# Sum of reciprocals: the input's rows laid out over the partitions in another way

## The chip, the cores and the metric

The kernel runs on one core of a Trainium2 chip. The metric is the device time of one execution in microseconds (us). Engines are named as in the profile: PE (TensorE), DVE (VectorE), ACT (ScalarE), POOL (GpSimd) and SP (SyncE), which here only issues DMAs. Sixteen DMA engines move data between the memory of the chip (DRAM) and the 128 partitions of the core's SBUF.

## The reference

```python
def setup_inputs():
    batch, seq, dim = 32, 512, 1024
    return {"x": np.abs(np.random.randn(batch, seq, dim)).astype(np.float32) + 1e-6}

def reference(x):
    return np.sum(1.0 / x, axis=-1).astype(np.float32)
```

There are 32 x 512 = 16,384 rows of 1,024 numbers, 4 KB each, 67.1 MB in all. The result is one number a row, 64 KB.

## The kernel before

Each partition handles 128 of the 16,384 rows. "Row r" below, from 0 to 127, means the r-th row of every partition, that is 128 rows of the input and 0.524 MB. The view `x_v` says which they are: partition p holds the 64 input rows from 64p on as its rows 0 to 63 (a = 0), and the 64 from 8192 + 64p on as its rows 64 to 127 (a = 1). So neighbouring partitions read addresses 256 KB apart, and `HALF` = 64 is a border that no transfer crosses.

SBUF has a ring of R = 46 slots of one row (`ring`). A load of rows goes into their slots as soon as the work on the rows that were there is done. The result of row r is column r of `sums`.

A reciprocal is the square of a reciprocal square root, and the work is spread over the engines in several ways. All that is done, and in which order on each engine, is written out by hand in `PLAN`, a list of tokens of a letter, a row, and a number of rows:

- `D10` loads the next 10 rows (line 169, SP). The tokens give 2, 10, 12, 12, 10 rows to fill the ring, then 10, 10, 10, 8, 8, 4, 5, 5, 4, 4, 3, 2, 2, 2, 1, 1, 1, 1 rows, and at last row 127 in two pieces of half a row.
- `A` is the reciprocal square root of whole rows, in place (line 177, ACT). `C` squares them on ACT, `Z` squares and sums on ACT (line 187), `G` squares on POOL (line 280), `Q` squares and sums on DVE (line 240), `T` sums on DVE (line 283), and `B`, `K`, `M` get the sum of squares from statistics on DVE (lines 255, 265, 270).
- `P`, `U`, `L`, `E`, `R` are a second way for some rows: POOL multiplies the two halves of a row (line 194), PE adds them (line 201), ACT takes the reciprocal square root of the products and squares it (line 211), and DVE multiplies and sums (line 220), since 1/a + 1/b = (a + b)/(ab).
- `O` issues the early stores of result columns (line 157, SP): columns 0 to 31, 32 to 63, 64 to 81, 82 to 98 and 99 to 115. The last store, columns 116 to 127, comes after the whole plan.

The D token that begins at row 56 asks for 10 rows; the loop over `m` cuts it at HALF into 8 and 2. So there are 26 load transfers and 6 stores, all on SP's queue, 32 in all. They take eight completion semaphores in turn, and a transfer waits on SP until the one that had its semaphore before has landed.

Of the kernel before, what the change touches and what calls it, by code (L numbers as in the profile page):

```python
# [11 lines left out]
def kernel(  # L12
# [5 lines left out]
    nc = tc.nc  # L18
    f32 = mybir.dt.float32
    P = 128  # L20
# [1 line left out]
    D = 1024  # L22
    H = D // 2
    F = 128
    HALF = F // 2
    R = 46
    NP = 5
    PIECES = ((127, 0, 512), (127, 512, 512))
    NR = 127
    STATS = ((55, 4, 16), (78, 4, 9),)  # L30
    STORES = (0, 32, 64, 82, 99, 116)
    LATE = ("A", 127)
    S = float(2**17)
    FIT = 1.0 - 2.0**-17
# [28 lines left out]
    mult = mybir.AluOpType.mult  # L63
    add = mybir.AluOpType.add

    x_v = x.flatten_outer_dims().rearrange("(a p f) d -> a p f d", a=2, p=P)
    out_v = out.flatten().rearrange("(a p f) -> a p f", a=2, p=P)

    act_sets = list(get_activation_tables(nc.m.arch).keys())
    nc.scalar.add_instruction(  # L70
# [13 lines left out]
    sums = pool.tile([P, F], f32)  # L84
# [12 lines left out]
    def place(u):  # L97
        return (u, 0, D) if u < NR else PIECES[u - NR]

    def area(u, n=1):  # L100
        r, at, w = place(u)
        if u >= NR:
            w, n = sum(place(i)[2] for i in range(u, u + n)), 1
        return ring[:, r % R : r % R + n, at : at + w]
# [48 lines left out]
    slot, bank = {}, {}  # L153

    def store(lo, hi):
        a, at = divmod(lo, HALF)
        nc.sync.dma_start(out=out_v[a, :, at : at + hi - lo], in_=sums[:, lo:hi])

    with tc.manual_schedule():
        for op, u, n, b in (parse(tok) for tok in PLAN):  # L160
            if op == "D":
                n, u = u, loaded
                while n:
                    r, at, w = place(u)
                    m = min(n, R - r % R, NR - u, HALF - r % HALF) if u < NR else n
                    k = m
                    if u >= NR:
                        w, k = sum(place(i)[2] for i in range(u, u + m)), 1
                    inst = nc.sync.dma_start(  # L169
                        out=area(u, m),  # L170
                        in_=x_v[r // HALF, :, r % HALF : r % HALF + k, at : at + w],
                    )
                    note("SP", inst, writes=rows(u, m))
                    u, n = u + m, n - m
                loaded = u
            elif op in "AC":
                inst = nc.scalar.activation(  # L177
                    out=area(u, n),
                    in_=area(u, n),
                    func=Arsqrt if op == "A" else Square,  # L180
                    scale=FIT if op == "A" else 1.0,
                )
                note("ACT", inst, writes=rows(u, n))
                work[op, u] = inst.ins
            elif op == "Z":
                r = place(u)[0]
                inst = nc.scalar.activation(  # L187
                    out=area(u), in_=area(u), func=Square, accum_out=sums[:, r : r + 1]
                )
                summed.add(r)  # L190
                note("ACT", inst, writes=rows(u))
            elif op == "P":
                slot[u], r = b, u % R
                inst = nc.gpsimd.tensor_tensor(  # L194
                    out=prod[:, b], in0=ring[:, r, :H], in1=ring[:, r, H:], op=mult
                )
                note("POOL", inst, rows(u), [("slot", b)])
            elif op == "U":
                bank[u], r = b, u % R
                for h in range(2):  # L200
                    inst = nc.tensor.matmul(  # L201
                        ps[:, b],
                        lhsT=ident,
                        rhs=ring[:, r, h * H : (h + 1) * H],
                        start=h == 0,
                        stop=h == 1,
                    )
                    note("PE", inst, half(u, h * H), [("bank", b)])
            elif op in "LE":
                pair = prod[:, slot[u]]  # L210
                inst = nc.scalar.activation(  # L211
                    out=pair,
                    in_=pair,
                    func=Arsqrt if op == "L" else Square,
                    scale=S * FIT if op == "L" else 1.0,
                )
                note("ACT", inst, writes=[("slot", slot[u])])
            elif op == "R":
                pair = prod[:, slot[u]]
                inst = nc.vector.tensor_tensor_reduce(  # L220
                    out=pair,
                    in0=pair,
                    in1=ps[:, bank[u]],
                    scale=S,
                    scalar=0.0,
                    op0=mult,
                    op1=add,
                    accum_out=sums[:, u : u + 1],
                )
                note("DVE", inst, [("bank", bank[u])], [("slot", slot[u])])  # L230
            elif op == "Q":
                r, at, w = place(u)
                joined = [u]
                while len(joined) < n:
                    joined += [i for i in range(NR, u) if place(i)[0] == r][-len(joined) :][:1]
                at -= sum(place(i)[2] for i in joined[1:])
                w += sum(place(i)[2] for i in joined[1:])
                row = ring[:, r % R, at : at + w]
                total = sums[:, r : r + 1]
                inst = nc.vector.tensor_tensor_reduce(  # L240
                    out=row,
                    in0=row,
                    in1=row,
                    scale=1.0,
                    scalar=total if r in summed else 0.0,
                    op0=mult,
                    op1=add,
                    accum_out=total,
                )
                summed.add(r)  # L250
                note("DVE", inst, writes=[s for i in joined for s in rows(i)])
            elif op == "B":
                i = stat_rows.index(u)
                for h in range(2):
                    inst = nc.vector.bn_stats(  # L255
                        out=stats[:, i, h], in_=ring[:, u % R, h * H : (h + 1) * H]
                    )
                    note("DVE", inst, reads=half(u, h * H), writes=[("stat", i)])
            elif op in "KM":
                lo, step, n = STATS[u]  # L260
                i = stat_rows.index(lo)
                part = stats[:, i : i + n]
                if op == "K":
                    mean = part[:, :, :, :, 1].rearrange("p f h e -> p (f h e)")
                    inst = nc.scalar.activation(  # L265
                        out=mean, in_=mean, func=Square, scale=float(H // 2) ** 0.5
                    )
                    engine = "ACT"
                else:
                    inst = nc.vector.tensor_reduce(  # L270
                        out=sums[:, lo : lo + step * (n - 1) + 1 : step],
                        in_=part[:, :, :, :, 1:].rearrange("p f h e k -> p f (h e) k"),
                        axis=mybir.AxisListType.XY,
                        op=add,
                    )
                    engine = "DVE"
                note(engine, inst, writes=[("stat", j) for j in range(i, i + n)])
            elif op == "G":
                row = area(u, n)
                inst = nc.gpsimd.tensor_tensor(out=row, in0=row, in1=row, op=mult)  # L280
                note("POOL", inst, writes=rows(u, n))
            elif op == "T":
                inst = nc.vector.tensor_reduce(  # L283
                    out=sums[:, u : u + n],
                    in_=area(u, n),
                    axis=mybir.AxisListType.X,
                    op=add,
                )
                note("DVE", inst, reads=rows(u, n))
            elif op == "O":  # L290
                for lo, hi in zip(STORES, STORES[1:]):
                    store(lo, hi)
        store(STORES[-1], F)
        for i in range(NOPS):
            inst = nc.gpsimd.nop(hint="idle", nofuse=True)
            if i == 0:
                tc.add_manual_dep(
                    inst.ins,
                    work[LATE].name,
                    mybir.DependencyInfo(  # L300
                        mybir.DependencyClass.Sync, mybir.DependencyReason.DATA
                    ),
                    reason="GpSimd idles behind the loads",
                )
# [30 lines left out]
```

## Time and profile before

| | |
|---|---|
| Time, median of 3 runs | 165.95 us (165.87 to 166.01) |
| Time of the profiled execution | 165.94 us |
| Span in its profile, first to last instruction | 164.2 us |
| Outside of the span | 1.74 us |
| Busy: ACT, DVE, POOL, PE | 148.9, 122.1, 97.2, 28.8 us |
| DMA queue of the loads and stores | 4,608 packets, 67.18 MB, 96.3% of 16 engines' span |
| Mean rate over the span | 409 GB/s |

The busy rows count an engine's own instructions; issuing a DMA counts as busy on no engine, and shows in the rows of SP's queue (SPq). A row of a source line gives an operation's shortest, median and longest duration in ns, and when the first and the last of them started. "DMA to landing" is the time from issue to the last byte. A row of the timeline gives start, duration, engine, line, operation and, in brackets, how long the engine was idle before it and what ended that.

### The profile page before, as it was taken

How to read it: one execution, taken by the hardware profiler on the slowest of the kernel's cores; microseconds unless marked ns; L12 is line 12 of the kernel's file. 1: busy time of each engine (PE TensorE's matmuls, PEld its weight loads, DVE VectorE, ACT ScalarE, POOL GpSimd, SP SyncE). 2: the span in 40 equal slices, each digit the busy share in tenths (PEclk: the TensorE clock that was granted, in tenths of full speed). 3: DMA queues.
4: the chain of work that ended last, by engine and by line, in shares of the span. 5: the costliest groups of instructions: out<-in, count | busy, mean ns of one | idle time of the engine just before them, and what ended most of it. 6: DMA issues, size and time to landing. Idle time of an engine off the chain costs nothing.

```text
span 164.2 us, 575 instructions
## 1 busy us (share of the span) xinstructions
PE 28.8 (18%) x48; PEld 10.3 (6%) x48; DVE 122.1 (74%) x148; ACT 148.9 (91%) x138; POOL 97.2 (59%) x47
## 2 busy tenths in 40 slices
PE   0000000000058000000000062000000077797700
PEld 0000000000022000000000020000000022232200
DVE  0000002599389996499999889979999999999994
ACT  3630799899999999999999999999999999999994
POOL 1000224924799399999999999674072695465400
PEclk9999999999999655555555559555555558999995
DMA  5979998899897999999899799999999999999970
GB/s 188 547 319 479 395 563 383 383 515 443 383 469 329 479 479 401 399 471 415 375 495 469 337 495 393 471 407 391 447 413 449 415 435 411 434 408 414 409 257 4
DMA packets 4611, 67.20 MB, mean 409 GB/s; under 512 B 1280, under 2 KB 1280, under 8 KB 2048
## 3 DMA queue, kind: packets, MB, share of 16 engines
q1 hardware_dynamic: 4608, 67.18, 96.3%
q14 instruction: 3, 0.02, 0.0%
HBM read 67.11 MB, written 0.07 MB: 409 GB/s over the span
## 4 chain that ended last, share of the span: by engine, by line
ACT 48%; DMA 42%; DVE 5%; POOL 2%; issue 1%; SPq 0%; DVEq 0%; POOLq 0%
DMA ring<-in_x_dram 42%; ACT ring L177 37%; ACT ring L187 6%; ACT prod L211 5%; DVE sums L283 3%; DVE ring L240 2%; POOL prod L194 2%; SPq L169 0%; DVE stats L255 0%; DVE prod L220 0%; ACT stats L265 0%; DVE sums L240 0%; DVEq L240 0%; POOLq L194 0%; DVEq L330 0%
## 5 line engine op out<-in xcount | busy, mean ns | idle before, releaser
L177 ACT ACTIVATE ring<-ring 128x1024 f32<-128x1024 f32 (+5 forms) x69 | 114.6, 1722 | 12.0 <-DMA ring<-in_x_dram 12.0
L280 POOL TENSOR_TENSOR ring<-ring 128x1024 f32<-128x1024 f32 (+3 forms) x29 | 81.1, 2820 | 48.1 <-ACT ring L177 48.1
L283 DVE TENSOR_REDUCE sums<-ring 128x1 f32<-128x1024 f32 (+3 forms) x30 | 56.8, 1920 | 31.2 <-ACT ring L177 30.9
L201 PE MATMUL ps<-ring,ident 128*128 128x512 f32 x48 | 28.8, 742 | 126.7 <-DMA ring<-in_x_dram 126.7
L240 DVE CUSTOM_DVE_ANT_0 ring<-ring 128x1024 f32<-128x1024 f32 (+1 forms) x20 | 28.8, 1450 | 5.9 <-ACT ring L177 5.8
L255 DVE BATCH_NORM_STATS2 stats<-ring 128x6 f32<-128x512 f32 x50 | 31.2, 680 | 2.6 <-ACT ring L177 2.5
L187 ACT ACTIVATE ring<-ring 128x1024 f32<-128x1024 f32 x21 | 21.9, 1041 | 0.0
L194 POOL TENSOR_TENSOR prod<-ring 128x512 f32<-128x512 f32 x12 | 15.6, 1308 | 9.0 <-DMA ring<-in_x_dram 9.0
L201 PEld LDWEIGHTS ps<-ring,ident 128*128 128x128 f32 x48 | 10.3, 231 | 144.3 <-DMA ring<-in_x_dram 86.5
L211 ACT ACTIVATE prod<-prod 128x512 f32<-128x512 f32 x24 | 14.2, 618 | 0.1
L220 DVE CUSTOM_DVE_ANT_0 prod<-prod,ps 128x512 f32<-128x512 f32 x12 | 7.9, 678 | 0.0
L187 ACT ACTIVATION_READ_ACCUMULATOR ring<-ring 128x1 f32 x21 | 3.9, 187 | 0.0
L70 ACT ACT_TABLE_LOAD x1 | 1.3, 1283 | 0.7 <-PEq L319 0.7
L240 DVE DVE_READ_ACCUMULATOR2_ANT sums<- 128x1 f32 x21 | 1.7, 81 | 0.0
L220 DVE DVE_READ_ACCUMULATOR2_ANT sums<- 128x1 f32 x12 | 1.0, 82 | 0.0
L240 DVE CUSTOM_DVE_ANT_0 ring<-ring,sums 128x512 f32<-128x512 f32 x1 | 0.8, 752 | 0.1
L265 ACT ACTIVATE stats<-stats 128x36 f32<-128x36 f32 (+1 forms) x2 | 0.5, 258 | 0.0
L270 DVE TENSOR_REDUCE sums<-stats 128x9 f32<-128x72 f32 (+1 forms) x2 | 0.5, 248 | 0.0
masks.py:197 POOL MEMSET ident<- 128x128 f32 x1 | 0.2, 205 | 0.3 <-POOLq L319 0.3
masks.py:199 POOL TENSOR_SCALAR_AFFINE_SELECT ident<-ident 128x128 f32<-128x128 f32 x1 | 0.3, 295 | 0.1
L319 POOL MEMSET const-float32-0.0<- 128x1 f32 x1 | 0.1, 99 | 0.2 <-issue 0.2
L319 POOL MEMSET const-bfloat16-1.0<- 128x1 bf16 x1 | 0.1, 102 | 0.0
(2 smaller groups left out, 0.2 us busy)
## 6 DMA issues: line engine op xcount, KB each, us to landing
ring<-in_x_dram SPq DMA_DIRECT2D x4, 5120.0 KB, 34.4
ring<-in_x_dram SPq DMA_DIRECT2D x2, 6144.0 KB, 37.5
ring<-in_x_dram SPq DMA_DIRECT2D x3, 4096.0 KB, 31.1
ring<-in_x_dram SPq DMA_DIRECT2D x3, 2048.0 KB, 35.9
ring<-in_x_dram SPq DMA_DIRECT2D x5, 1024.0 KB, 33.1
ring<-in_x_dram SPq DMA_DIRECT2D x2, 2560.0 KB, 35.2
ring<-in_x_dram SPq DMA_DIRECT2D x4, 512.0 KB, 21.7
ring<-in_x_dram SPq DMA_DIRECT2D x1, 1536.0 KB, 40.3
```

What stands on the lines that cost most here:

```text
L70: nc.scalar.add_instruction(mybir.InstLoadActFuncSet(name=nc.get_next_instruction_name(), act_func_set_id=act_sets.index("abs_reciprocal_s ...
L177: inst = nc.scalar.activation(out=area(u, n), in_=area(u, n), func=Arsqrt if op == "A" else Square, scale=FIT if op == "A" else 1.0,)
L187: inst = nc.scalar.activation(out=area(u), in_=area(u), func=Square, accum_out=sums[:, r : r + 1])
L194: inst = nc.gpsimd.tensor_tensor(out=prod[:, b], in0=ring[:, r, :H], in1=ring[:, r, H:], op=mult)
L201: inst = nc.tensor.matmul(ps[:, b], lhsT=ident, rhs=ring[:, r, h * H : (h + 1) * H], start=h == 0, stop=h == 1,)
L211: inst = nc.scalar.activation(out=pair, in_=pair, func=Arsqrt if op == "L" else Square, scale=S * FIT if op == "L" else 1.0,)
L220: inst = nc.vector.tensor_tensor_reduce(out=pair, in0=pair, in1=ps[:, bank[u]], scale=S, scalar=0.0, op0=mult, op1=add, accum_out=sums[:, ...
L240: inst = nc.vector.tensor_tensor_reduce(out=row, in0=row, in1=row, scale=1.0, scalar=total if r in summed else 0.0, op0=mult, op1=add, acc ...
L255: inst = nc.vector.bn_stats(out=stats[:, i, h], in_=ring[:, u % R, h * H : (h + 1) * H])
L265: inst = nc.scalar.activation(out=mean, in_=mean, func=Square, scale=float(H // 2) ** 0.5)
L280: inst = nc.gpsimd.tensor_tensor(out=row, in0=row, in1=row, op=mult)
L283: inst = nc.vector.tensor_reduce(out=sums[:, u : u + n], in_=area(u, n), axis=mybir.AxisListType.X, op=add,)
```

## The change

The view of the input becomes `(l e f) d -> e l f d` with l = 8, e = 16 and f = 128. The input is seen as 128 pieces of 128 sequent rows (512 KB); partition 8e + l holds piece 16l + e. So the eight partitions 8e to 8e + 7 read pieces that lie 16 pieces (8 MB) apart, and partitions that differ by 8 read pieces next to each other. The output's view is changed alike. The source of a load has now two counted dimensions (16 and 8) ahead of the contiguous run, where it had one (128); the destination is as before.

With the border at row 64 gone, the D token at row 56 is one transfer of 10 rows, which leaves 25 load transfers. The early stores are cut in steps of `PART` = 20 columns up to `DONE` = 116, six in place of five. Loads and stores together stay 32. `PLAN` is the same.

```diff
-    HALF = F // 2
...
-    STORES = (0, 32, 64, 82, 99, 116)
+    DONE = 116
+    PART = 20
...
-    x_v = x.flatten_outer_dims().rearrange("(a p f) d -> a p f d", a=2, p=P)
-    out_v = out.flatten().rearrange("(a p f) -> a p f", a=2, p=P)
+    x_v = x.flatten_outer_dims().rearrange("(l e f) d -> e l f d", l=8, e=P // 8)
+    out_v = out.flatten().rearrange("(l e f) -> e l f", l=8, e=P // 8)
...
     def store(lo, hi):
-        a, at = divmod(lo, HALF)
-        nc.sync.dma_start(out=out_v[a, :, at : at + hi - lo], in_=sums[:, lo:hi])
+        nc.sync.dma_start(out=out_v[:, :, lo:hi], in_=sums[:, lo:hi])
...
-                    m = min(n, R - r % R, NR - u, HALF - r % HALF) if u < NR else n
+                    m = min(n, R - r % R, NR - u) if u < NR else n
...
                     inst = nc.sync.dma_start(
-                        out=area(u, m),
-                        in_=x_v[r // HALF, :, r % HALF : r % HALF + k, at : at + w],
+                        out=area(u, m), in_=x_v[:, :, r : r + k, at : at + w]
                     )
...
             elif op == "O":
-                for lo, hi in zip(STORES, STORES[1:]):
-                    store(lo, hi)
-        store(STORES[-1], F)
+                for c in range(0, DONE, PART):
+                    store(c, min(c + PART, DONE))
+        store(DONE, F)
```

## Prediction

> **What bounds the kernel now.** I read the busy line and the DMA rows of the page first, then the waits of ScalarE (ACT), then the table of stages, then the issue rows of SyncE (SP). The page says that two things are nearly full: the DMA queue and ACT.
>
> ```profile
> PE 28.8 (18%) x48; PEld 10.3 (6%) x48; DVE 122.1 (74%) x148; ACT 148.9 (91%) x138; POOL 97.2 (59%) x47
> ...
> q1 hardware_dynamic: 4608, 67.18, 96.3%
> ```
>
> The reader sees ACT busy for 148.9 of 164.2 us and the 16 DMA engines for 96.3% of the span. Which of them sets the end is told by ACT's first 33 us and its list of waits:
>
> ```profile
> 5.51 1.91 ACT L177 ACTIVATE ring<-ring 128x2048 f32<-128x2048 f32 x1 [3.50 <-DMA ring<-in_x_dram]
> ...
> 17.61 10.91 ACT L177 ACTIVATE ring<-ring 128x2048 f32<-128x2048 f32 x6 [7.96 <-DMA ring<-in_x_dram]
> ...
> 32.15 1.06 ACT L177 ACTIVATE ring<-ring 128x1024 f32<-128x1024 f32 x1 [0.52 <-DMA ring<-in_x_dram]
> ```
> ```profile
> ACT ring L177 <- DMA ring<-in_x_dram: 12.0, 3, 8.0
> ACT L70 <- PEq L319: 0.7, 1, 0.7
> ```
>
> ACT waits for a load three times, for transfers 1 (2 rows), 2 (10 rows) and 3 (12 rows), and never after 32.15. From there it works without a gap to the end: 161.78 - 32.15 = 129.6 us. So a thing that moves the first three landings moves the end by the same amount, and a thing that happens to the loads later costs nothing until they fall behind ACT. They are not far ahead. Here is the table of stages:
>
> ```profile
> 17.60:32.10 14.50, 0.00 (x0) 0.00 (x0) 3.41 (x2) 14.03 (x12) 7.30 (x2) 1.00 1.00 434
> 32.10:60.00 27.90, 5.96 (x8) 2.34 (x8) 23.43 (x20) 27.85 (x21) 18.74 (x9) 0.91 1.00 432
> 60.00:100.00 40.00, 3.73 (x4) 1.18 (x4) 34.93 (x29) 39.97 (x34) 39.66 (x14) 0.51 0.99 425
> 100.00:145.00 45.00, 10.24 (x19) 3.93 (x20) 43.76 (x63) 44.96 (x42) 25.59 (x15) 0.62 1.00 425
> ```
>
> The columns are the stretch, its length, then busy time of PE, PEld, DVE, ACT and POOL, the granted clock, the DMA share and GB/s. The DMA share is 0.99 to 1.00 at 425 to 434 GB/s all the way: ten rows of 0.524 MB land in 17.61 - 5.51 = 12.10 us, 1.21 us a row, or 433 GB/s. The last two pieces, issued at 146.0 and 148.4, need 13.2 and 11.5 us to land, so the last one is there at 159.9, and ACT's last four ARSQRTs (A125 to A128) run back to back:
>
> ```profile
> 157.71 3.03 ACT L177 ACTIVATE ring<-ring 128x1024 f32<-128x1024 f32 x4
> ```
>
> They end at 160.74, and A128, a half row of about 0.6 us, starts at 160.1. So the stream leaves ACT some 0.2 us there. Both are at their limit together.
>
> The third limit is what lies outside both, at the start and at the end: SP's issue.
>
> ```profile
> L169 SPq DMA_DIRECT2D ring<-in_x_dram x26: 327/328/652, 0.7 to 148.4; - x26
> ...
> DMA to landing us min/median/max: 4.8/33.3/56.0
> ```
> ```profile
> L169 SPq DMA_DIRECT2D ring<-in_x_dram x5: 383/427/652, 0.7 to 2.8; - x5
> ```
> ```profile
> L157 SPq DMA_DIRECT2D out_dram<-sums x6: 332/332/348, 150.9 to 161.9; - x6
> L157 SPq EVENT_SEMAPHORE  x4: 17/17/3392, 153.4 to 158.5; - x4
> ...
> DMA to landing us min/median/max: 1.4/5.2/9.1
> ```
>
> The durations are minimum, median and maximum in ns; the middle row is the first five loads alone. The first load goes out at 0.74 and lands 4.8 us later; the last store goes out at 161.92 and lands 1.4 us later. The profiled execution took 165.94 us, of which 164.2 are the span and 1.74 lie around it; the median is 165.95, so sums are made on 165.94. A measurement of this kernel can tell about 0.2% (0.33 us) from no change.
>
> **Part 1: the row transfers read a pattern of one dimension more.** A transfer's source was 128 partitions at one pitch (256 KB), and is now 16 pieces of 512 KB (e) by 8 steps of 8 MB (l). The bytes, the destination, the contiguous run per partition (4 KB a row) and the 128 descriptors stay. What can change is the price of an issue on SP and the rate of the stream.
>
> Issue: no row shows this pattern. The nearest rows are the same instruction on the plain pattern, from 327 ns to 652 ns, so the price of an issue lies between no change and +0.32 us; a gain I exclude, as the pattern only becomes harder. I take the dear end, 652 ns, since most issues here (the median is 328, within 1 ns of the least) look like a short form for a plain pattern and the 652 shows what the same instruction can cost when it is not in that form. Of the 25 load issues nearly all are covered: a load waits in the queue behind others (12.3 to 40.3 us to landing in the page's issue rows, the first transfer aside), so 0.3 us on SP disappear there. If that cover went, 0.3 us each would come on top. Two issues are not covered. The first load, now 383 ns (the least of the first five), moves its landing and with it the whole stream and ACT: +0.27. Transfers 2 to 5 are issued while transfer 1 runs, so they only have to be there by 5.1 us, when it is nearly through; five issues of 0.65 end at 4.0.
>
> Stream: by the rows it runs at one rate in every stage, and a descriptor of 4 KB or more has no reason in this trace to move faster or slower. I take 0. Its bounds are in the rivals.
>
> **Part 2: one transfer less.** The plan's D10 at row 56 was cut at 64 into 8 + 2 rows. Joined, it saves one set of 128 descriptors. An estimate from the table: 100 to 145 ran at 425 instead of 433 GB/s, 1.8% of 45 us = 0.83 us over some 13 landings, 0.06 us each; 60 to 100 gives 0.74 us over 4, 0.18. So 0.06 to 0.18 us in the stream at 81 us, where ACT doesn't wait: 0. Rows 56 to 63, which landed by themselves, are now told of together with 64 and 65, up to 2.4 us later (two rows of 1.21). Row 66 is complete at 32.1 + 42 x 1.21 = 82.9, and their first use is ACT's A56+5, three instructions of which start here:
>
> ```profile
> 83.95 9.90 ACT L177 ACTIVATE ring<-ring 128x5120 f32<-128x5120 f32 x3
> ```
>
> So work on earlier rows covers it by 1 us, and I cost it at nothing; without that cover it would be 2.4 us at most.
>
> **Part 3: six early stores for five, one last.** 128 + 128 + 72 + 68 + 68 bytes a partition become five of 80 and one of 64: the same bytes, 128 descriptors more, one issue more. Load and store transfers stay 32 in all (26 + 6, 25 + 7). They are issued from 150.9 on and stand in the queue behind the loads; SP then waits 3.39 us (158.5 to 161.9) for the last sums. One more issue of at most 0.65 us, and six dearer ones (6 x 0.32 = 1.9 us), fit into those 3.39 us, and no engine waits for an early store. The last store moves 12 columns as before, but its issue is on the path: 332 to 652 ns, +0.32. Its landing stays 1.4 us less 0.33 of issue; the target is now 512 bytes apart instead of 256, which I cost at 0.
>
> **Sum:** 165.94 + 0.27 + 0.32 = 166.53, so 166.5. With the bounds of the issue price this case reaches from 165.9 to 166.6.
>
> **Rivals.** *Nothing changes:* the issue is as short as before, the engines share the rows out as before, and what is saved is hidden: 165.9. For it: no row shows any issue of a harder pattern. Against it: it needs the median of 328 to hold for a new pattern. This is also the case in which the change doesn't do what it says (the engines don't read neighbouring pieces).
>
> *Faster, a shorter start:* the first transfer lands 4.8 us after issue. The last store shows 1.4 us for a landing of almost no data, and two rows at 1.21 are 2.42, so 0.98 us is lost while sixteen engines open their first pieces. Pieces next to each other may open faster. Half of it gives 165.45, all of it 165.0. It decides if the first ACT wait ends before 5.5. Against: the same 0.98 can be the fill of the queue, whatever the addresses.
>
> *Slower, the read side:* at the same time the engines now also have descriptors in flight that lie 8 MB apart. If that takes the rate of the whole stream from 433 to 425 GB/s, as the slower stages of the table show it for other reasons, the 158 us from 1.7 to 159.9 become 161.0; less the 0.2 us of slack that is 168.7. It decides once the stream is 0.2 us late. [...] This trace, at 256 KB, shows no loss at all.
>
> *Slower, the write side:* with the slow dimension 16 instead of 128, a DMA engine may be given eight neighbouring partitions, where it may have had another set before. If two engines then write through one entrance of SBUF in turn, each has half of the rate of 27 GB/s (433 / 16) that it has now. That doubles 158 us at worst: 324; if they drift apart it is less, and 180 is possible. For it: 433 GB/s in every stage says that no two engines share anything today, so the present split could only get worse. Against: nothing in the trace shows such an entrance. [...]
>
> **How the numbers follow.** The forecast (dearer issues) gets 0.40, of which 0.37 above 0.2%. Nothing changes: 0.20 (0.18 same, 0.02 faster). Shorter start: 0.20 (0.17 faster, 0.03 same). Read side: 0.06. Write side: 0.14. Slower is 0.37 + 0.06 + 0.14 = 0.57, same 0.03 + 0.18 + 0.03 = 0.24, faster 0.19. The range from 165.3 to 169.0 holds the forecast, no change, most of the shorter start and the read side's mild form, about 0.82; the write side is left out, as it would stretch the range to 324. The forecast's own range is 165.9 to 166.6.
>
> **What would show it.** Right: load and store issues with a median of about 0.65 us; ACT's three waits ending about 0.27 later (5.78, 17.9, 32.4); 432 to 434 GB/s in the early stages; the last store's issue at 162.2 and taking 0.65. Wrong: an issue median near 328 (then no change, or the start decides, to be read off the first ACT wait); a rate under 430 between 17 and 60 us, with more and longer ACT waits for the loads than three.

## The result and the profile after

The changed kernel takes nearly twice as long: a median of 325.82 us against 165.95, and a ratio of 1.947 with a 95% interval of 1.935 to 1.959 (the ratio leaves out executions that were disturbed, the median doesn't). The profiled execution took 323.64 us, with a span of 321.9. The forecast of 166.5 us, and its range of 165.3 to 169.0, missed by far; the rival named "the write side", with 324 us, is what came.

The page of the changed kernel, busy line and DMA queue:

```profile
PE 33.1 (10%) x48; PEld 11.5 (4%) x48; DVE 122.0 (38%) x148; ACT 151.2 (47%) x138; POOL 96.6 (30%) x47
...
q1 hardware_dynamic: 4608, 67.18, 98.3%
```

The engines do the same work as before (ACT 151.2 us against 148.9) in a span of twice the length. The queue has the same 4,608 packets and the same bytes, and its engines are still busy all the time: 98.3% of a span that is twice as long. So every packet takes about twice as long: share times 16 engines times span, divided by the packets, is 1.10 us where it was 0.55.

ACT's first loads (ACT's timeline) and its waits:

```profile
7.83 1.91 ACT L175 ACTIVATE ring<-ring 128x2048 f32<-128x2048 f32 x1 [5.81 <-DMA ring<-in_x_dram]
...
32.85 10.91 ACT L175 ACTIVATE ring<-ring 128x2048 f32<-128x2048 f32 x6 [20.89 <-DMA ring<-in_x_dram]
...
62.99 4.56 ACT L175 ACTIVATE ring<-ring 128x1024 f32<-128x1024 f32 x2 [16.12 <-DMA ring<-in_x_dram]
```
```profile
ACT ring L175 <- DMA ring<-in_x_dram: 167.0, 24, 20.9
```

Ten rows now land in 32.85 - 7.83 = 25.0 us instead of 12.1, and ACT, which waited three times for 12.0 us in all, waits 24 times for 167.0 us. The difference of 155 us is almost the whole loss of 157.7 between the two profiled executions. The table of stages (stretch, length, busy time of PE, PEld, DVE, ACT and POOL, clock, DMA share, GB/s):

```profile
62.40:118.00 55.60, 5.60 (x8) 2.23 (x8) 24.72 (x24) 27.68 (x20) 21.20 (x8) 0.87 0.98 205
118.00:193.00 75.00, 0.00 (x0) 0.00 (x0) 29.26 (x21) 36.51 (x30) 32.78 (x11) 0.50 0.99 208
193.00:297.00 104.00, 19.29 (x28) 6.74 (x28) 51.68 (x74) 53.58 (x50) 29.22 (x17) 0.60 1.00 213
297.00:317.00 20.00, 8.26 (x12) 2.53 (x12) 11.47 (x24) 11.99 (x17) 3.81 (x3) 0.67 1.01 233
```

The rate is 205 GB/s where 12 and 10 rows go in one transfer and rises to 233 where single rows do; before it was 434 to 425. The issue rows of loads and stores:

```profile
L168 SPq DMA_DIRECT2D ring<-in_x_dram x25: 536/537/664, 0.7 to 298.2; - x25
...
DMA to landing us min/median/max: 7.1/75.5/114.7
```
```profile
L156 SPq DMA_DIRECT2D out_dram<-sums x7: 538/538/587, 302.8 to 319.3; - x7
...
DMA to landing us min/median/max: 1.8/6.7/14.9
```

An issue has become dearer, 537 ns instead of 328, as the forecast had it (at up to 652). That is real, but it is a few tenths of a microsecond. What had been put at nothing, the stream, costs the rest, about 157.

### The profile page after: what moved, and what is told of

Read it like the earlier page. It is cut to its first block, busy times and chain, and to the rows that moved or that the text cites. A ratio compares the mean times of both kernels' runs of the same rounds, so it can differ in the third digit from the quotient of the medians.

```text
span 321.9 us, 575 instructions
## 1 busy us (share of the span) xinstructions
PE 33.1 (10%) x48; PEld 11.5 (4%) x48; DVE 122.0 (38%) x148; ACT 151.2 (47%) x138; POOL 96.6 (30%) x47
## 3 DMA queue, kind: packets, MB, share of 16 engines
q1 hardware_dynamic: 4608, 67.18, 98.3%
## 4 chain that ended last, share of the span: by engine, by line
another core or an unknown queue 51%; ACT 29%; DMA 16%; SPq 2%; DVE 1%; ACTq 0%; issue 0%
ACT ring L175 23%; DMA ring<-in_x_dram 16%; ACT ring L185 4%; SPq L168 2%; DVE sums L281 1%; ACT prod L209 1%; DVE stats L253 0%; ACTq L328 0%
## 5 line engine op out<-in xcount | busy, mean ns | idle before, releaser
L175 ACT ACTIVATE ring<-ring 128x1024 f32<-128x1024 f32 (+5 forms) x69 | 115.3, 1726 | 167.0 <-DMA ring<-in_x_dram 167.0
L199 PE MATMUL ps<-ring,ident 128*128 128x512 f32 x48 | 33.1, 841 | 276.8 <-DMA ring<-in_x_dram 276.8
L238 DVE CUSTOM_DVE_ANT_0 ring<-ring 128x1024 f32<-128x1024 f32 (+1 forms) x20 | 27.2, 1362 | 75.2 <-ACT ring L175 75.2
L199 PEld LDWEIGHTS ps<-ring,ident 128*128 128x128 f32 x48 | 11.5, 258 | 297.1 <-DMA ring<-in_x_dram 189.1
```

Source lines behind the costliest of these rows:

```text
L175: inst = nc.scalar.activation(out=area(u, n), in_=area(u, n), func=Arsqrt if op == "A" else Square, scale=FIT if op == "A" else 1.0,)
L199: inst = nc.tensor.matmul(ps[:, b], lhsT=ident, rhs=ring[:, r, h * H : (h + 1) * H], start=h == 0, stop=h == 1,)
L238: inst = nc.vector.tensor_tensor_reduce(out=row, in0=row, in1=row, scale=1.0, scalar=total if r in summed else 0.0, op0=mult, op1=add, acc ...
```

## The experiments

The theories were these. W, the write side: a source of 16 by 8 gives each DMA engine the eight neighbouring partitions 8e to 8e + 7, and then two engines write through one entrance of SBUF at a time. (An entrance is this theory's word for what two writers would share; no row of a profile shows one.) R, the read side: the pieces collide in DRAM because of their distances. F, later: a source with two counted dimensions makes the DMA engines slow, whatever they write.

**The same pieces by one counted dimension, and other pieces by two.** Four kernels were compared. The first takes the changed kernel and gives up only the split (partition p holds piece p, and the view of the output is changed alike):

```diff
-    x_v = x.flatten_outer_dims().rearrange("(l e f) d -> e l f d", l=8, e=P // 8)
+    x_v = x.flatten_outer_dims().rearrange("(p f) d -> p f d", p=P)
...
```

> Partition p holds piece p of 128 sequent rows: the same 128 pieces of 512 KB as in the changed kernel, also 25 loads and 6 early stores, but the source of a load has one counted dimension (128) as before. Theory W (write side: a source of 16 by 8 gives each DMA engine eight neighbouring partitions, and two engines then share one entrance of SBUF): as fast as before, 165.6 to 166.3 us, issues of 328 ns. Theory R (read side: the larger and wider-spaced pieces collide in DRAM): clearly slower, over 180 us. If the loss came from 25 loads, 6 early stores or the pieces' size, it would be about 325 here too.

It took 167.12 us, ratio 1.0072 (1.0048 to 1.0096). The factor of two is gone. So neither the 25 transfers, nor the 6 early stores, nor pieces of 512 KB make it. But my interval ended at 166.3, and this is 0.7% slower than before, clear of noise: there is a small price of its own, on which more below.

The second goes the other way: the kernel before, with neighbouring partitions 256 KB apart, but with a hole after every eighth, so that the source can't be written with one counted dimension.

```diff
-    x_v = x.flatten_outer_dims().rearrange("(a p f) d -> a p f d", a=2, p=P)
+    x_v = x.flatten_outer_dims().rearrange("(e a l f) d -> a e l f d", a=2, e=16, l=8)
...
```

> The kernel before with its 26 loads and 5 early stores, and again neighbouring partitions 256 KB apart, but a source that can't be written with one counted dimension: partition 8e + l holds rows 1024e + 64l on, and 512 rows further for its second half, so a load counts 16 by 8. Nothing of a partition's eight neighbours is 8 MB away. W: as slow as the change, 310 to 330 us, issues of 537 ns, 10 rows in 25 us. R, as far as 8 MB steps are its cause: 166 to 175 us.

It took 323.42 us, ratio 1.948 (1.943 to 1.952), as slow as the change, with the transfers of before and neighbours again 256 KB apart. Third and fourth, all loads read inside 8 MB, once by 16 by 8 and once by 128:

```diff
-    x_v = x.flatten_outer_dims().rearrange("(l e f) d -> e l f d", l=8, e=P // 8)
+    x_v = x.flatten_outer_dims()[: 16 * P].rearrange("(l e f) d -> e l f d", l=8, e=P // 8)
...
+                    v = min(r % 16, 16 - k)
...
-                        out=area(u, m), in_=x_v[:, :, r : r + k, at : at + w]
+                        out=area(u, m), in_=x_v[:, :, v : v + k, at : at + w]
```

> The changed kernel with pieces of 16 rows in place of 128: all loads read inside the first 8 MB of the input, again and again (so most of the input is left out and the sums are not the reference's); the source still counts 16 by 8, and partition 8e + l holds piece 16l + e, steps of 64 KB and 1 MB. W: 310 to 330 us. R: near 166 us, or at least far from 325, since the distances are an eighth.

> The control of the run with pieces of 16 rows: the same 8 MB, partition p holds piece p, so one counted dimension (again most of the input is left out). W: 165.6 to 166.6 us. If reading the same 8 MB again and again is slow in itself, it shows here.

They took 325.18 us (ratio 1.958, 1.952 to 1.965) and 166.09 us (ratio 1.0002, 0.9992 to 1.0013). R falls as the cause of the factor: with 256 KB, 1 MB or 8 MB between neighbours the time is the same 323 to 326, and it hangs on 16 by 8 against 128 alone. The last of the four also has 25 loads and 6 early stores, and it ties with before: that part of the change costs and brings nothing that can be measured.

**Loads alone, by the shape of the source.** W and F both explain this much. A kernel of seven loads of 10 rows, each waiting for the one before, tells them apart.

```diff
...
+    load(out=ring[:, :10], in_=one)      # L25: 128
+    load(out=ring[:, :10], in_=two)      # L26: 16 by 8
+    load(out=ring[:, :10], in_=holes)    # L27: 128 by 10
+    load(out=ring[:, :10], in_=two32)    # L28: 32 by 4
+    load(out=ring[:, :10], in_=two64)    # L29: 64 by 2
+    load(out=ring[:, :10], in_=two)      # L30: 16 by 8
+    load(out=ring[:, :10], in_=one)      # L31: 128
...
```

> Loads alone, one after the other, each waiting for the one before, 10 rows (5.24 MB) to all 128 partitions; all sums are left out. Sources by counted dimensions: 128; 16 by 8; 128 by 10 (rows with gaps, 4 KB runs); 32 by 4; 64 by 2; 16 by 8 again; 128 again. A landing at 433 GB/s takes 12.1 us and some 2 us from issue to the first data, so about 14. Theory W (who writes where; the slow dimension alone decides it, and anything but 128 gives an engine eight neighbours): 128 takes 14, 128 by 10 takes 14 to 15, and 16 by 8, 32 by 4 and 64 by 2 all take 26 to 28. Theory F (a source with two counted dimensions makes the DMA engines slower whatever they write): 128 by 10 takes 26 to 28 as well.

SP's timeline of this kernel; the start of a row less the start of the row above it is what the load above took:

```profile
0.73 0.38 SPq L25 DMA_DIRECT2D ring<-in_x_dram  x1
15.89 0.65 SPq L26 DMA_DIRECT2D ring<-in_x_dram  x1
43.73 0.39 SPq L27 DMA_DIRECT2D ring<-in_x_dram  x1
59.60 0.58 SPq L28 DMA_DIRECT2D ring<-in_x_dram  x1
74.44 0.55 SPq L29 DMA_DIRECT2D ring<-in_x_dram  x1
89.92 0.56 SPq L30 DMA_DIRECT2D ring<-in_x_dram  x1
117.69 0.34 SPq L31 DMA_DIRECT2D ring<-in_x_dram  x1
132.71 0.35 SPq L32 DMA_DIRECT2D out_dram<-ring  x1
```

128 takes 15.2 and 15.0 us, 16 by 8 takes 27.8 twice, 128 by 10 takes 15.9: F falls, since that one has two counted dimensions too and 4 KB runs besides. But 32 by 4 takes 14.8 and 64 by 2 takes 15.5. I had expected 26 to 28 for them, so W in its first form (anything but 128 deals out whole blocks) is too wide: with a slow dimension of 32 or 64 a load is as fast as by 128, within 0.5 us, and with 16 it is not. The rows also split what I had thought one thing: the issue is dear (0.55 to 0.65 us) for all three with a split partition dimension, and the stream is slow for one of them.

**The entrances.** Do some partitions get in each other's way and others not, as W has it? Plain sources, a few chosen partitions, 160 KB to each:

```diff
...
+    load(out=ring[0:2], in_=flat[0:2, :N])            # L21: partitions 0, 1
+    load(out=ring[0:5:4], in_=flat[0:5:4, :N])        # L22: 0, 4
+    load(out=ring[0:9:8], in_=flat[0:9:8, :N])        # L23: 0, 8
+    load(out=ring[0:33:32], in_=flat[0:33:32, :N])    # L24: 0, 32
+    load(out=ring[0:65:64], in_=flat[0:65:64, :N])    # L25: 0, 64
+    load(out=ring[0:8], in_=flat[0:8, :N])            # L26: 0 to 7
+    load(out=ring[0:29:4], in_=flat[0:29:4, :N])      # L27: 0, 4, ... 28
+    load(out=ring[0:57:8], in_=flat[0:57:8, :N])      # L28: 0, 8, ... 56
+    load(out=ring[0:113:16], in_=flat[0:113:16, :N])  # L29: 0, 16, ... 112
...
```

> Loads alone, plain sources, each waiting for the one before; all sums are left out. After one full load, 160 KB go to each of a few chosen partitions, each of which should get a DMA engine of its own: 160 KB at 27 GB/s take 6.05 us, with some 2 us to the first data 8 us. Theory W, with entrances of two groups of four partitions 32 apart: partitions 0 and 1: 14 us; 0 and 4: 8; 0 and 8: 8; 0 and 32: 14; 0 and 64: 8; 0 to 7: 26 (four engines at each of two entrances); 0, 4, ... 28: 8; 0, 8, ... 56: 14; 0, 16, ... 112: 14. Theory F (entrances don't matter, the form of the source does): all nine take 8 us.

SP's timeline again, differences of starts as above:

```profile
52.41 0.31 SPq L21 DMA_DIRECT2D ring<-in_x_dram  x1
66.23 0.77 SPq L22 DMA_DIRECT2D ring<-in_x_dram  x1
75.27 0.62 SPq L23 DMA_DIRECT2D ring<-in_x_dram  x1
83.47 0.51 SPq L24 DMA_DIRECT2D ring<-in_x_dram  x1
97.37 0.51 SPq L25 DMA_DIRECT2D ring<-in_x_dram  x1
106.14 0.29 SPq L26 DMA_DIRECT2D ring<-in_x_dram  x1
131.57 0.74 SPq L27 DMA_DIRECT2D ring<-in_x_dram  x1
140.72 0.59 SPq L28 DMA_DIRECT2D ring<-in_x_dram  x1
156.61 0.59 SPq L29 DMA_DIRECT2D ring<-in_x_dram  x1
172.34 0.38 SPq L30 DMA_DIRECT2D out_dram<-ring  x1
```

| Partitions | us | At one entrance, by W |
|---|---|---|
| 0, 1 | 13.8 | 2 |
| 0, 4 | 9.0 | 1 |
| 0, 8 | 8.2 | 1 |
| 0, 32 | 13.9 | 2 |
| 0, 64 | 8.8 | 1 |
| 0 to 7 | 25.4 | 4 |
| 0, 4, ... 28 | 9.2 | 1 |
| 0, 8, ... 56 | 15.9 | 2 |
| 0, 16, ... 112 | 15.7 | 2 |

All nine come out in the class that W gave them, within 2 us of the time expected. At the 27 GB/s of one stream (in the packet records of the kernel before, 40 KB take 1.51 us) 160 KB take 6.05 us, and the loads that W puts one, two and four to an entrance take about 2.1 to 3.1, 1.7 to 3.8 and 1.2 us more than one, two and four times that. So partitions 0 and 1 (13.8 us), and 0 and 32 (13.9), take the time of two streams one after the other, 0 and 4, 0 and 8, and 0 and 64 (9.0, 8.2 and 8.8) that of two side by side, and 0 to 7 (25.4) that of four in a row. That entrances make it is what W assumes; the run shows the times of these nine loads, and they agree with it. The chosen partitions also read addresses apart from each other, by 0.5, 2, 4, 16 and 32 MB in the first five loads; that 0.5 and 16 are slow (13.8 and 13.9 us) and 2, 4 and 32 fast (9.0, 8.2 and 8.8) fits W and no order of distances.

**Which engine gets which block.** By W, with the pairs as measured, if block e of eight partitions goes to one engine in full, blocks 0 to 3 meet nobody, and blocks 4 to 7, which lie 32 partitions further on, meet them. Loads by sources of 16, 2, 4, 8, 4, 8 and 16 blocks by 8:

```diff
...
+    load(out=ring[:, :10], in_=two[:, :, :10])         # L21: 16 blocks
+    load(out=ring[0:16, :10], in_=two[0:2, :, :10])    # L22: 2
+    load(out=ring[0:32, :10], in_=two[0:4, :, :10])    # L23: 4
+    load(out=ring[0:64, :10], in_=two[0:8, :, :10])    # L24: 8
...
+    load(out=ring[:, :10], in_=two[:, :, 10:20])       # L27: 16
...
```

> Loads alone, each waiting for the one before, all sums left out: the first 16, 2, 4, 8, 4, 8 and 16 blocks of eight partitions, by sources of so many by 8, 10 rows to a partition. Theory W, if block e goes to DMA engine e in full: an engine moves 8 x 40 KB in every one of them (12.1 us at its full rate, about 15 with the start). With the entrances of two groups of four, 32 partitions apart, that the runs on chosen partitions showed, blocks 0 to 3 meet nobody and blocks 4 to 7 the entrances of blocks 0 to 3. So 2 and 4 blocks: 14 to 16 us; 8 blocks: 26 to 28; 16 blocks: 26 to 28. If an engine doesn't get one block, or the form 'so many by 8' is slow in itself, 4 blocks are as slow as 8.

```profile
0.73 0.67 SPq L21 DMA_DIRECT2D ring<-in_x_dram  x1
28.57 0.76 SPq L22 DMA_DIRECT2D ring<-in_x_dram  x1
43.54 0.67 SPq L23 DMA_DIRECT2D ring<-in_x_dram  x1
58.49 0.63 SPq L24 DMA_DIRECT2D ring<-in_x_dram  x1
85.88 0.64 SPq L25 DMA_DIRECT2D ring<-in_x_dram  x1
100.68 0.62 SPq L26 DMA_DIRECT2D ring<-in_x_dram  x1
128.28 0.59 SPq L27 DMA_DIRECT2D ring<-in_x_dram  x1
156.02 0.36 SPq L28 DMA_DIRECT2D out_dram<-ring  x1
```

Two blocks take 15.0 us, four 15.0 and 14.8, eight 27.4 and 27.6, sixteen 27.8 and 27.7. The same form of source is fast with two and four blocks and slow with eight and sixteen; by W, the second set then meets the first. If a block goes to one engine, an engine moves the same 320 KB in every one of these loads, 12.1 us at 27 GB/s (an estimate). The rows of the DMA queue in the windows of the first load of four blocks and the first of eight show how long a packet of theirs took:

```profile
q1 hardware_dynamic: 36, 1.31, 21.8%
```
```profile
q1 hardware_dynamic: 72, 2.62, 45.1%
```

Of these packets 32 and 64 are the 40 KB for one partition, the others a few bytes. Share times 16 engines times window gives 52.1 us of packet time in 14.95 us and 197.6 us in 27.39, which is 1.63 us for a packet with four blocks and 3.09 us with eight. The single packet records of the two whole kernels say much the same: 40 KB take 1.51 us before (median of 512, the least too), and 3.17 in the changed kernel (of 640, the least 2.95). (The three kernels of loads alone were executed once each; loads of one form within them agree to about 0.2 us.) With the run on chosen partitions this fits W: two engines stand at one entrance, write four partitions there, and go on to the next entrance together. That picture is my explanation of the times. Which engine gets which block isn't in the records, and that it is one block to an engine is an estimate, from the 15.0 us of two blocks against the 12.1 of 320 KB.

**One transfer in the kernel before.** Only the 10 rows at row 56 are read by 16 by 8:

```diff
-                        in_=x_v[r // HALF, :, r % HALF : r % HALF + k, at : at + w],
...
+                    if 56 <= u < 66:
+                        src = x_s[r // HALF, :, :, r % HALF : r % HALF + k, at : at + w]
```

> The kernel before with one change: the 10 rows at row 56 (8 + 2) are read with a source of 16 by 8 (so other rows go to the partitions, and the order of those results differs). W: the loss sits in each transfer, so these rows land 10 x (2.50 - 1.21) = 12.9 us later, ACT, which was 0.5 to 1 us behind the loads there, waits about 12.4 us once, and the end moves by as much: 177.5 to 179.5 us. If the stream only slows as a whole when all transfers are split, it stays near 166. If there is more slack than my prediction's 0.2 to 1 us, it is less than 177.

It took 179.42 us, ratio 1.081 (1.079 to 1.083): 13.4 us for ten rows, just inside the upper end of the interval. ACT's timeline has the loss where it was expected, at rows 56 and after:

```profile
92.36 4.47 ACT L179 ACTIVATE ring<-ring 128x5120 f32<-128x5120 f32 x1 [7.51 <-DMA ring<-in_x_dram]
97.31 5.56 ACT L179 ACTIVATE ring<-ring 128x5120 f32<-128x5120 f32 x2 [0.48 <-DMA ring<-in_x_dram]
...
109.14 8.16 ACT L179 ACTIVATE ring<-ring 128x1024 f32<-128x1024 f32 x4 [4.19 <-DMA ring<-in_x_dram]
```

It isn't one wait but three of 12.2 us together, as the rows were cut in 8 and 2 and rows behind them came late too. The loss sits in the transfer, and the end pays it in full: the prediction's view of the slack was right.

**The price of the issue alone.** The kernel before, with only the stores' destination counted 16 by 8:

```diff
-    out_v = out.flatten().rearrange("(a p f) -> a p f", a=2, p=P)
+    out_v = out.flatten().rearrange("(e a l f) -> a e l f", a=2, e=16, l=8)
...
```

> The kernel before, its loads untouched; only the destinations of the six stores count 16 by 8 (the results land in another order than the reference's). My term for the dearer issue of the last store was +0.32 us; the changed kernel's stores took 538 ns instead of 332, so now +0.21 us is expected, 166.1 to 166.4, and no more, if few bytes don't notice a shared entrance. If the store's own writes suffer, over 166.5.

It took 166.44 us, ratio 1.0024 (1.0015 to 1.0033), which is +0.25 to +0.55 us and a shade over the interval expected. The stores of this kernel:

```profile
L157 SPq DMA_DIRECT2D out_dram<-sums x6: 538/539/625, 151.1 to 162.1; - x6
...
DMA to landing us min/median/max: 1.8/5.1/9.1
```

The issue took 0.21 us more, and the last store landed 1.8 us after it began instead of 1.4: the landing comes later by more than the issue itself. So the term is 0.4 rather than the 0.21 of this expectation, or the 0.32 of the prediction.

**The change by 32 by 4 and 64 by 2.** The loads alone had shown that 32 by 4 keeps the stream fast (14.8 us). So the changed kernel was run with 4 in place of 8 in both of its views; partitions that differ by 4 now read pieces next to each other.

```diff
-    x_v = x.flatten_outer_dims().rearrange("(l e f) d -> e l f d", l=8, e=P // 8)
+    x_v = x.flatten_outer_dims().rearrange("(l e f) d -> e l f d", l=4, e=P // 4)
...
```

> The changed kernel with 32 by 4 in place of 16 by 8: partition 4e + l holds piece 32l + e, so engines still read pieces next to each other and a partition's neighbour is 16 MB away; 25 loads, 6 early stores, two counted dimensions. Theory W as the loads alone have narrowed it (a slow dimension of 32 is still dealt out in groups of four partitions, one entrance to an engine; 16 is not): the stream is back at 430 GB/s and what is left is the price of the dearer issue, first load and last store, 2 x 0.2 to 0.4 us: 166.3 to 166.9 us. If far steps in DRAM cost (theory R), more: over 167.5. If pieces next to each other open faster at the start, under 166.2.

> The same with 64 by 2: partition 2e + l holds piece 64l + e, the neighbour 32 MB away. W: as with 32 by 4, 166.3 to 166.9 us. R: over 167.5 us. Shorter start: under 166.2.

32 by 4 took 166.63 us, ratio 1.0041 (1.0025 to 1.0056); 64 by 2 took 167.83, ratio 1.0109 (1.0094 to 1.0125). Issue rows and first waits with 32 by 4:

```profile
L168 SPq DMA_DIRECT2D ring<-in_x_dram x25: 534/535/667, 0.7 to 149.2; - x25
```
```profile
5.57 1.91 ACT L175 ACTIVATE ring<-ring 128x2048 f32<-128x2048 f32 x1 [3.55 <-DMA ring<-in_x_dram]
...
17.79 10.90 ACT L175 ACTIVATE ring<-ring 128x2048 f32<-128x2048 f32 x6 [8.10 <-DMA ring<-in_x_dram]
...
32.48 1.06 ACT L175 ACTIVATE ring<-ring 128x1024 f32<-128x1024 f32 x1 [0.67 <-DMA ring<-in_x_dram]
```

The third landing is at 32.48 instead of 32.15. The first transfer is hardly later (5.57 for 5.51) in spite of the dearer issue, so a part of it may come back at the start. With 64 by 2 the second landing is at 18.68 instead of 17.61, and there the expectation of 166.3 to 166.9 missed. Its table of stages has the loss between the first two landings:

```profile
5.50:17.60 12.10, 0.00 (x0) 0.00 (x0) 0.00 (x0) 4.10 (x5) 0.00 (x0) 1.00 0.94 391
```

The kernel before and 32 by 4 have 444 GB/s in this stretch. The load of 64 by 2 alone, which took 15.5 us, had shown no such loss. Whether the steps of 32 MB make it or something else, no run separates. None of the versions beats the kernel before.

## Why the prediction was wrong, step by step

*What bounds the kernel.* This held. Stream and ACT were both at their limit, with tenths of a microsecond between them, so the lost rate reached the end almost in full: 155 us more of ACT's waits, 157.7 us more of time. The run with one split transfer measures the same: 13.4 us lost for 12.9 expected at the landing.

*Part 1, the issue.* Right in kind and nearly in size: 383 to 664 ns for the first load (+0.28 for +0.27), 332 to 538 for the last store (+0.21 for +0.32), with some 0.2 us more until the data moves: the first packet of the trace starts at 2.17 us instead of 1.74, and the last store lands 1.8 us after its issue begins instead of 1.4. With the stream out of the way, at 32 by 4, the change comes to +0.68 us (0.42 to 0.93) for the +0.59 of the sum. So 166.5 would have been the answer to a neighbour of this change. Some of that nearness is luck. The 652 ns, taken as the price of a pattern that isn't plain, was the issue of a load like all others, the fourth one:

```profile
L169 SPq DMA_DIRECT2D ring<-in_x_dram x1: 652/652/652, 2.1 to 2.1; - x1
```

With 512 KB pieces in one counted dimension one issue took 830 ns. The price of the pattern is the median of 537, and the first load's 664 came out near 652 by chance.

*Part 1, the stream.* This is the step that failed: "I take 0". The reason given there, that a descriptor of 4 KB or more has no reason in the trace to move faster or slower, looked at the descriptor alone. What it left out is what the other engines write at the same time. A 40 KB packet took 3.17 us instead of 1.51, as with two at one entrance by W, so that 1.21 us a row became 2.50, and that is about 157 of the 157.7 us lost.

*The rival that came.* Its mechanism, as an assumption, its price (324 us) and a sign of it (a rate under 430 GB/s with many more waits of ACT) were on record, at a chance of 0.14. What was held against it, that "nothing in the trace shows such an entrance", was no evidence: a layout that never makes two engines meet can't show an entrance, so the row would be missing in either case. What spoke for it was in the same paragraph: 425 to 434 GB/s in every stage is sixteen streams of 27 (a sixteenth of the rate), with no sign of a disturbance, and nothing on record said that the new form of source keeps them apart. The loads alone show that it doesn't keep the rate: 27.8 us by 16 by 8, 15.2 and 15.0 by 128.

*The read side.* Not the cause of the factor, and not nothing: 512 KB from partition to partition cost 0.7% with one counted dimension, where the run inside 8 MB, with 64 KB from partition to partition, lost nothing, while 32 by 4, with 16 MB from partition to partition, costs nothing that could be told from the price of its issues. Nor did the 16 MB steps of 32 by 4 slow the stream for good: it ran at 410 GB/s from 32 to 60 us and at 429 and 430 from there to 145, where the kernel before had 432, 425 and 425. Why 512 KB costs its 0.7% and 64 by 2 its 1.1% was not settled.

*Parts 2 and 3.* One transfer less and one early store more cost nothing, as costed: the run inside 8 MB with one counted dimension has both, and a ratio of 1.0002.

*The shorter start.* Not seen in the time: ACT's first wait ends at 5.57 us with 32 by 4, at 5.51 before, and at 5.62 and 5.65 in two more profiles with plain loads (the 512 KB pieces, and the stores alone by 16 by 8). From issue to landing the first load took 4.8 us with 32 by 4, as before, though no issue of a load was under 534 ns there and the first one before took 383. So the opening may have been a tenth or two of a microsecond shorter (my estimate from these rows) and paid for a part of the dearer issue; it is one profile, and with 64 by 2 the landing took 5.1 us.

## What to carry to other kernels

Here a load at full rate was sixteen streams of 27 GB/s, and 16 by 8 in place of 128 halved them, while other steps between the addresses in DRAM cost at most the 1.1% of 64 by 2: when the outermost dimension of a load's source changes, ask first which partitions each DMA engine may write and whether any two of them may get in each other's way, and only then what the addresses in DRAM do. That a trace shows no sign of a shared resource is no evidence against it if the kernel's layout never makes two engines share it; give such a rival its chance by how well its condition is met, and try it with a few loads alone. If rows have to be spread over partitions by two dimensions, 32 by 4 kept the rate here (166.63 us) and 16 by 8 halved it (325.82).

## What the runs showed of the hardware that I had not expected

- A load of 5.24 MB by a source of 32 by 4 or 64 by 2 takes 14.8 and 15.5 us, close to the 15.2 and 15.0 by 128; by 16 by 8 it takes 27.8.
- By 16 by 8 the stream has about half of its rate: 205 GB/s with transfers of 10 and 12 rows, 233 with single rows, for 433 before. Why the first is under half and the second over it was not settled.
- The issue costs 537 ns instead of 328 where the partitions are counted in two dimensions, and a store by such a pattern lands 0.4 us later (1.8 us after it begins, for 1.4), 0.21 of it in the issue. A source of 128 by 10 had a short issue (0.39 us). Loads to chosen partitions with a step between them had long ones (0.51 to 0.77 us, against 0.29 and 0.31 without a step), with one counted dimension.
